# A hybrid attention and RG-LRU block: another order in the opening, with c spread by a transfer and the first shift summed on VectorE

## The chip, the cores and the metric

The kernel runs on one core of a Trainium2 chip. A core has TensorE (PE, matrix products), VectorE (DVE), ScalarE (ACT), GpSimd (POOL) and SyncE (SP, which here only issues transfers), and 16 DMA engines between its memory (SBUF) and HBM. The metric is the device time of one launch in microseconds.

## The reference, cut to what matters

```python
def rmsnorm(x, g):
    r = lax.rsqrt(jnp.mean(xf * xf, axis=-1, keepdims=True) + NORM_EPS)
    return (xf * r).astype(x.dtype) * g
...
    mod = c @ w_ada[l] + b_ada[l]                    # c: 1 x 1024
    shift, scale, gate = jnp.split(mod, 3, axis=-1)
    h = rmsnorm(x, norm_g[l]) * (1.0 + scale[:, None, :]) + shift[:, None, :]
    proj = h @ w_in[l]
    q, k, v, g_attn, xr, g_rnn, m_attn, m_rnn = jnp.split(proj, SPLIT_POINTS, axis=-1)
    ...  # rotary positions, windowed attention with sinks, convolution, RG-LRU
    merged = (jax.nn.sigmoid(m_attn) * (y_attn @ w_attn_proj[l])
              + jax.nn.sigmoid(m_rnn) * (y_rnn @ w_rnn_proj[l]))
    x = x + gate[:, None, :] * (merged @ w_out[l])
return rmsnorm(x, final_g)
```

x is 1024 rows (time) by 1024 features. The change concerns the way from x and c to h, and the first products that use h.

## The kernel before, in words

Products are made in three passes: each operand is split into a high part (a value rounded to the reduced matmul format) and a low part (the rest), and high by high, low weight by high, and high weight by low are added up. In names, `wh`/`wl` are the parts of a weight half, `hh`/`hl` those of h; `hha`/`hhb` are the two time halves of a chunk of `hh`. The products of the main projection that come after the opening use sums and differences of quarter blocks of h (`differences`, `make_operands`, the operands `nh` and `nl`) and run in line 690.

The opening works in this order. `manual_schedule` means that every engine executes its instructions exactly in program order; an instruction that waits holds up all behind it on its engine.

- Loads, on SyncE's queue in program order: the eight 128-row tiles of x (`xt`, 512 KB each), the packed small parameters `pk_t`, then halves of weights (`r`, 256 KB) and tiles of the shift and scale weights (`wada`, 512 KB, two for each of the eight 128-feature chunks of h) in the order of their use. `xt` and `wada` share 12 buffers. The two halves of the row c (`c_row_t`, 2 KB each) come on ScalarE's queue.
- TensorE is kept turning with products of zeros (`turn_array`, line 251), then spreads c over the 128 partitions by a product with a column of ones (line 259); VectorE copies that to `c_bc` (lines 420, 421).
- For each x tile i: `square(i)` sums the squares on ScalarE (line 360, with an accumulator read behind it), `mean(i)` divides and adds epsilon on VectorE (363), `root(i)` is on ScalarE (367), `scaled(i)` inverts on VectorE (371) and multiplies either the tile (373) or, for tiles 0, 2 and 4, an identity matrix (377). `flip(i)` transposes the tile's eight chunks on TensorE (lines 390 and 392) into one of two sets of four PSUM banks; two tiles share a set.
- `out_of(j, p, eng)` evicts bank p of tile pair j into `xT` (line 398 on ScalarE, 400 on VectorE). Pairs 0 and 2 are in one set of banks (`bk`), 1 and 3 in the other (the later accumulators `pmain`).
- The first chunk's shift is a sum over features by eight thin products (line 446, on weights laid out for that on the host), all other shifts and all scales are multiply-and-sum instructions on VectorE (`modulate`, line 270). Four more products of zeros follow (449, `KEEP_BUSY`).
- `scales_of(kc)` makes the two per-feature constants of chunk kc on ScalarE (275, 277). `hi_parts(kc)` makes from `xT` the high part in two halves (406; whole in 408 for chunks 4 to 7) and the full value (410) on ScalarE, with what is given as `between` in the middle. `lo_parts(kc)` makes the low part on VectorE (467, 470). `cast_s` and `rest_s` split the weight halves of the first four output blocks (101 on ScalarE or 219 on GpSimd, and 107 on VectorE).
- `first(kc, terms, cs)` multiplies chunk kc into the accumulators of the output blocks cs, in line 480: term "h" is high by high, "w" low weight by high, "l" high weight by low. The first products of all are those of chunk 0.

Behind the eight chunks, lines 1488 to 1523 interleave the last low parts, the differences and operands for the main products, the halves of the v weights (`half`), the rotary positions of the keys (`rope_a`, `rope_b`), which read and free the first accumulators, and two products for v (`v_product`, lines 1461 to 1463). GpSimd computes the angles of the rotary positions in small steps (`turn`).

Of the kernel before, what the change touches and what calls it, by code (L numbers as in the profile page):

```python
# [12 lines left out]
F32 = mybir.dt.float32  # L13
# [3 lines left out]
BF16 = mybir.dt.bfloat16  # L17
AF = mybir.ActivationFunctionType
ALU = mybir.AluOpType
# [26 lines left out]
SL = [slice(0, HALF), slice(HALF, S)]  # L46
XT = 12
DIAG = 0, 2, 4
KEEP_BUSY = 4


@with_exitstack
def tile_hybrid_block(ctx, tc, x, pk, rows, posr, posi, c_row, w_ss, w_gate, w_main, w_v,
# [32 lines left out]
    def pcol(base, i):  # L86
        return pk_t[:, base + i:base + i + 1]
# [97 lines left out]
    START = (0, 1, 34, 35)  # L185
    with ExitStack() as st:
        sp = st.enter_context(tc.tile_pool(name="start", bufs=1, side="right"))
        c_row_t = [wp.tile([P, HALF], F32, tag="ws", name="c_row_t", bufs=3)[0:1, :]
                   for _ in range(2)]
        for i in range(2):  # L190
            dma(c_row_t[i], c_row[:, SL[i]], A)
        posr_t = sp.tile([P, 65], I32, name="posr_t")
        dma(posr_t[:], posr, G)
        invf_t = posr_t[:, 64:65].bitcast(F32)
# [3 lines left out]
        for i in range(8):  # L198
            t = sp.tile([P, D], F32, tag="xt", name="xt", bufs=XT)
            dma(t[:], x[i * P:(i + 1) * P, :])  # L200
            xt.append(t)
        dma(pk_t[:], pk)

        def load_ss(kc):
# [18 lines left out]
        def rest_s(c, i):  # L223
            rest(sw[c][i], raw[c, i])
# [15 lines left out]
            load_ss(kc)  # L240
        rv = [load_half(w_v[i // 2][:, SL[i % 2]]) for i in range(4)]

        one_row = sp.tile([1, P], F32, name="one_row")
        warm = sp.tile([P, 1], F32, name="warm")
        V.memset(one_row[:], 1.0)
        zero = rbig[:, :HALF]
        V.memset(zero, 0.0)

        def turn_array(n):
            for i in range(n):  # L250
                T.matmul(bk[i % 2], zero[:, 0:P], zero, start=True, stop=True)  # L251

        V.memset(warm[:], 1.0)
        A.activation(warm[:], warm[:], AF.Sqrt)
        c_bc = sp.tile([P, D], F32, name="c_bc")
        psc = starts[0]
        turn_array(12)
        for hf in range(2):
            T.matmul(psc[hf], one_row[:], c_row_t[hf], start=True, stop=True)
        turn_array(2)  # L260

        mods = sp.tile([P, 16], F32, name="mods")
        gsc = sp.tile([P, 8], F32, name="gsc")
        shf = sp.tile([P, 8], F32, name="shf")
        bng = sp.tile([P, 8], F32, name="bng")

        def modulate(kc, which=(0, 1)):
            for a in which:
                jk = sp.tile([P, D], BF16, tag="junk2", name="jk")
                V.scalar_tensor_tensor(out=jk[:], in0=wada[kc, a][:], scalar=1.0, in1=c_bc[:],  # L270
                                       op0=ALU.mult, op1=ALU.mult,
                                       accum_out=mods[:, a * 8 + kc:a * 8 + kc + 1])

        def scales_of(kc):
            A.activation(shf[:, kc:kc + 1], mods[:, kc:kc + 1] if kc else bk[0][:, 0:1],
                         AF.Identity, bias=pcol(PK_BSH, kc))
            A.activation(gsc[:, kc:kc + 1], mods[:, 8 + kc:9 + kc], AF.Identity,
                         scale=pcol(PK_NG, kc), bias=bng[:, kc:kc + 1])

# [77 lines left out]
        junk_t = wp.tile([P, HALF], F32, tag="ws", name="junk", bufs=3)  # L357

        def square(i):
            A.activation(junk_t[:].bitcast(BF16), xt[i][:], AF.Square, accum_out=ss[:, i:i + 1])  # L360

        def mean(i):
            V.tensor_scalar(out=rr[:, i:i + 1], in0=ss[:, i:i + 1], scalar1=1.0 / D, scalar2=EPS,
                            op0=ALU.mult, op1=ALU.add)

        def root(i):
            A.activation(rr[:, i:i + 1], rr[:, i:i + 1], AF.Sqrt)

        def scaled(i):
            r1 = rr[:, i:i + 1]  # L370
# [49 lines left out]
        late = {1: [lambda: V.tensor_copy(c_bc[:, SL[0]], psc[0]),  # L420
                    lambda: V.tensor_copy(c_bc[:, SL[1]], psc[1])],
                3: [lambda: out_of(0, 0, V), lambda: out_of(0, 1, V)],
                4: [lambda: out_of(0, 2, V), lambda: out_of(0, 3, A)],
                5: [lambda: out_of(1, 0, V), lambda: out_of(1, 1, V)],
                6: [lambda: out_of(1, 2, A), lambda: out_of(1, 3, A),
                    lambda: V.scalar_tensor_tensor(
                    out=bng[:], in0=pk_t[:, PK_BSC:PK_BSC + 8], scalar=1.0,
                    in1=pk_t[:, PK_NG:PK_NG + 8], op0=ALU.add, op1=ALU.mult)]}
        for i in range(8):
            square(i)  # L430
            mean(i)
            if i:
                root(i - 1)
                scaled(i - 1)
                if i < 6:
                    turn(3)
                flip(i - 1)
            for f in late.get(i, ()):
                f()
        root(7)  # L440
        scaled(7)
        for p in range(4):
            out_of(2, p, A)
        flip(7)
        for k in range(KC):
            T.matmul(bk[0][:, 0:1], wada[0, 0][:, k * P:(k + 1) * P], pcol(PK_C, k),
                     start=(k == 0), stop=(k == KC - 1))
        for i in range(KEEP_BUSY):
            T.matmul(bk[1], zero[:, 0:P], zero, start=True, stop=True)
# [12 lines left out]
        csn = sp.tile([P, 3, 64], F32, name="csn")  # L462
# [28 lines left out]
        def more():  # L491
            out_of(3, 2, A)
            out_of(3, 3, A)
# [1005 lines left out]
    now(rope_a(lambda: starts[0][0], 0, to_k))  # L1499
    for c in range(2, 4):  # L1500
        for kc in (6, 7):
# [360 lines left out]
def arrange(inputs):  # L1862
    i = {k: np.asarray(v) for k, v in inputs.items()}
    w_in = i["w_in"][0]
    w_ada = i["w_ada"][0]
    b_ada = i["b_ada"][0]
    cw = i["conv_w"][0]
    a = {}
    a["x"] = np.ascontiguousarray(i["x"][0])
    a["pk"] = np.ascontiguousarray(np.concatenate(  # L1870
        [_pc(i["c"][0]), _pc(b_ada[:1024]), _pc(b_ada[1024:2048]), _pc(i["norm_g"][0])]
        + [_pc(cw[k]) for k in range(4)]
        + [_pc(i["conv_b"][0]), _pc(i["rg_ba"][0]), _pc(i["rg_bx"][0]), _pc(i["rg_lambda"][0])],
        axis=1))
# [9 lines left out]
    a["w_ss"][:128] = w_ada[:, :128].reshape(8, 128, 128).transpose(1, 0, 2).reshape(128, 1024)  # L1884
# [25 lines left out]
```

## Time and profile before

| | us |
|---|---|
| median of 3 runs | 927.20 |
| lowest and highest | 926.62, 927.23 |
| the profiled execution | 927.22 |
| its span, first to last instruction | 925.4 |
| TensorE busy in it | 916.5 |
| VectorE, ScalarE, GpSimd busy | 677.7, 544.2, 128.9 |
| first product of line 480 starts at | 23.44 |

The profile is of one execution. Its page gives the busy time of each engine and the costliest groups of instructions; questions to the trace give the instructions of a stretch in order of time (start, duration, engine, line, operation, output <- inputs, and in brackets the idle time before it with what ended it), who waited for whom, and sums over given stretches. A duration includes what an engine overlaps with its next instruction, so two neighbours can start closer together than the first one's duration.

### The profile page before, as it was taken

To read this page: it belongs to the slowest core of one execution; us is meant where nothing else is said; L and a number is where in the kernel's file an instruction comes from. 1 tells how busy PE (TensorE), PEld (TensorE's weight loads), DVE (VectorE), ACT (ScalarE), POOL (GpSimd) and SP (SyncE) were. 2 spreads that over 40 slices of the span, in tenths; PEclk is the share of its full clock that TensorE was granted. 3 is DMA by queue.
4 is the path that set the end of the run, shared out by engine and by line. 5 is a ranking of instruction groups with operands and counts; after the bars stand their busy time and mean duration, and the time that the engine had idled before them with its cause. 6 is when DMAs were issued, how large, how long until landed. Compare 5 with 4: busy or idle time off the path is not lost.

```text
span 925.4 us, 12505 instructions
## 1 busy us (share of the span) xinstructions
PE 916.5 (99%) x4318; PEld 757.0 (82%) x4319; DVE 677.7 (73%) x1000; ACT 544.2 (59%) x1056; POOL 128.9 (14%) x225
## 2 busy tenths in 40 slices
PE   9999999999999999999999999999999999999997
PEld 6789888888888888888888888888888788888886
DVE  6997685877659946876786787899999748656522
ACT  7956654645558664956585875888887522212311
POOL 6420332000000000000000001444353200000000
PEclk9999999999999999999999999999999999999999
DMA  9829377641334522363334367994754198545331
GB/s 359 320 84 284 117 233 236 201 148 63 100 111 142 193 87 91 117 202 92 114 125 148 103 223 267 339 371 167 236 180 154 62 375 308 181 151 197 98 131 69
DMA packets 79300, 166.04 MB, mean 179 GB/s; under 512 B 7891, under 2 KB 28387, under 8 KB 79237
## 3 DMA queue, kind: packets, MB, share of 16 engines
q1 hardware_dynamic: 75152, 152.38, 47.5%
q0 software_dynamic: 3936, 12.59, 4.4%
q8 instruction: 34, 0.56, 0.2%
q14 instruction: 30, 0.24, 0.1%
q10 hardware_dynamic: 148, 0.27, 0.1%
HBM read 114.00 MB, written 51.61 MB: 179 GB/s over the span
## 4 chain that ended last, share of the span: by engine, by line
PE 94%; DVE 4%; issue 1%; ACT 1%; POOL 0%; DVEq 0%; ACTq 0%
PE bk L690 47%; PE rp L168 13%; PE pmain L1764 5%; PE pgate L1003 5%; PE pmain L168 5%; PE rp L1764 4%; PE s_ps L1214 3%; PE bk L480 3%; PE pv L1287 2%; PE pmain L480 2%; PE pt L1253 1%; PE pmain L1461 1%; PE pmain L1462 1%; PE pmain L1463 1%; PE bk L251 1%
## 5 line engine op out<-in xcount | busy, mean ns | idle before, releaser
L690 PE MATMUL bk<-nh,wh 128*128 128x512 f32 x368 | 144.5, 393 | 0.0
L690 PE MATMUL bk<-nl,wh 128*128 128x512 f32 x368 | 144.1, 392 | 0.0
L690 PE MATMUL bk<-nh,wl 128*128 128x512 f32 x368 | 143.8, 391 | 0.0
L101 ACT CAST wh<-r 128x512 fp32r<-128x512 f32 x107 | 65.7, 618 | 38.3 <-DMA r<-w_ap 15.4
L107 DVE TENSOR_TENSOR wl<-r,wh 128x512 fp32r<-128x512 f32 x109 | 79.0, 732 | 6.3 <-ACT wh L101 6.3
L690 PEld LDWEIGHTS bk<-nl,wh 128*128 128x128 f32 x368 | 69.1, 188 | 15.5
L690 PEld LDWEIGHTS bk<-nh,wl 128*128 128x128 f32 x368 | 69.1, 188 | 15.1
L690 PEld LDWEIGHTS bk<-nh,wh 128*128 128x128 f32 x368 | 69.2, 188 | 14.6
L690 PE MATMUL bk<-hh,wh 128*128 128x512 f32 x184 | 72.2, 393 | 0.0
L690 PE MATMUL bk<-hl,wh 128*128 128x512 f32 x184 | 72.1, 392 | 0.0
L690 PE MATMUL bk<-hh,wl 128*128 128x512 f32 x184 | 71.9, 391 | 0.0
L107 DVE TENSOR_TENSOR wl<-ws,wh 128x512 fp32r<-128x512 f32 x76 | 51.5, 684 | 4.8 <-ACT wh L101 4.8
L1239 ACT ACTIVATE p<-p,small 128x129 f32<-128x129 f32 x128 | 50.1, 401 | 0.0
L101 ACT CAST wh<-ws 128x512 fp32r<-128x512 f32 x76 | 45.7, 615 | 3.1 <-DVE ws L712 1.5
L690 PEld LDWEIGHTS bk<-hl,wh 128*128 128x128 f32 x184 | 34.6, 188 | 7.8
L690 PEld LDWEIGHTS bk<-hh,wl 128*128 128x128 f32 x184 | 34.6, 188 | 7.5
L690 PEld LDWEIGHTS bk<-hh,wh 128*128 128x128 f32 x184 | 34.6, 188 | 7.3
L1214 PE MATMUL s_ps<-ks,qs 128*128 128x256 f32 (+1 forms) x256 | 37.6, 289 | 0.1
L868 POOL MEMSET xr<- 128x3 f32 x8 | 0.8, 101 | 259.7 <-PE pgate L1003 233.0
L803 ACT ACTIVATE c<-bk 128x512 f32<-128x512 f32 x29 | 17.3, 597 | 32.6 <-PE bk L690 32.6
L690 PE MATMUL bk<-hha,wl 128*128 128x512 f32 x92 | 36.1, 393 | 0.2 <-DVE wl L107 0.2
L690 PE MATMUL bk<-hha,wh 128*128 128x512 f32 x92 | 36.1, 393 | 0.0
(365 smaller groups left out, 2283.3 us busy)
## 6 DMA issues: line engine op xcount, KB each, us to landing
r<-w_main SPq DMA_DIRECT2D x100, 256.0 KB, 4.2
wada<-w_ss SPq DMA_DIRECT2D x16, 512.0 KB, 9.1
qs<-q_d SPq DMA_DIRECT2D x16, 512.0 KB, 5.5
ks<-k_d SPq DMA_DIRECT2D x12, 384.0 KB, 3.5
xt<-x SPq DMA_DIRECT2D x8, 512.0 KB, 6.9
sma_d<-c SPq DMA_DIRECT2D x16, 256.0 KB, 3.3
q_d<-rhi SPq DMA_DIRECT2D x16, 256.0 KB, 4.0
q_d<-rlo SPq DMA_DIRECT2D x16, 256.0 KB, 4.2
```

The lines of the kernel that those rows point to most:

```text
L101: A.copy(dst[0][:], src)
L107: V.tensor_tensor(out=dst[1][:], in0=src, in1=f32(dst[0][:]), op=ALU.subtract)
L168: mm = T.matmul(ps[hf], ww, xx[kc][hf], start=(kc == 0 and ww is w_h and xx is xh), stop=(kc == KC - 1 and xx is xl))
L251: T.matmul(bk[i % 2], zero[:, 0:P], zero, start=True, stop=True)
L480: T.matmul(starts[c][hf], ww[:, c0:c0 + P], xh[kc][hf], start=(kc == 0 and t_ == "h"), stop=(kc == KC - 1 and t_ == "l"))
L690: W["pe"] = T.matmul(ps, ww[:, c], b[kc][xx_], start=(first and kc == 0 and i == 0), stop=(kc == 3 and i == 2), skip_group_check=not first)
L803: A.activation(t["t"], s(), AF.Tanh, scale=0.5)
L1003: W["pe"] = T.matmul(ps[:, SL[hf]], ww[:, c0:c0 + P], xx_[:, SL[hf]], start=(ic == 0 and i == 0), stop=(ic == 1 and i == 2))
L1214: W["pe"] = T.matmul(o, qs[:, j, qc], ks[:, kb:n % 2 + 2, b, :], start=(b == 0), stop=(b == 1))
L1239: A.activation(px[:, j, :], px[:, j, :], AF.Exp, bias=sm[:, 0, j:j + 1], accum_out=sm[:, 1, j:j + 1])
L1287: W["pe"] = T.matmul(pv[:], b, m[:].rearrange("p j q -> p (j q)"), start=(i == 0), stop=(i == len(prods) - 1))
L1764: T.matmul(ps[:, sl], lhs[k][th][:, ts_], w[:, sl], start=(k == 0 and w is h_ and lhs is mh), stop=(k == KC - 1 and lhs is ml))
```

## The change

`c` comes as one transfer that spreads its row over the partitions (512 KB into SBUF, on SyncE's queue behind x); the thin transfers, the products with ones and the two copies go. `mean` goes; `root` takes 1/D as its scale and a tile of epsilon as its bias. Tile 3 is squared on VectorE. Chunk 0's shift is summed by `modulate` like the others, with the weights in their usual layout, and the eight thin products go. `KEEP_BUSY` is 11 instead of 4. The loop over x tiles is written out: each root stands right behind its square, and evictions stand elsewhere; all four of pair 3 come ahead of the first `hi_parts`, and the casts of blocks 0 and 1 both stand inside it. The first products go through chunks 0 and 1 in another order. Later, `make_operands(0)` stands behind `lo_parts(7)`, and `differences(1)` behind the last half of v's weights. In the written-out part several statements share a line here.

```diff
-KEEP_BUSY = 4
+KEEP_BUSY = 11
+ON_V = 3,
...
-        for i in range(2):
-            dma(c_row_t[i], c_row[:, SL[i]], A)
...
+        c_bc = sp.tile([P, D], F32, name="c_bc")
+        dma(c_bc[:], c_row.to_broadcast([P, D]))
         dma(pk_t[:], pk)
...
-        V.memset(warm[:], 1.0)
-        A.activation(warm[:], warm[:], AF.Sqrt)
-        turn_array(12)
-        for hf in range(2):
-            T.matmul(psc[hf], one_row[:], c_row_t[hf], start=True, stop=True)
-        turn_array(2)
+        V.memset(warm[:], EPS)
+        A.activation(mods[:, 0:1], warm[:], AF.Sqrt)
+        turn_array(16)
...
         def square(i):
+            if i in ON_V:
+                jk = sp.tile([P, D], BF16, tag="junk2", name="jk")
+                V.scalar_tensor_tensor(out=jk[:], in0=xt[i][:], scalar=1.0, in1=xt[i][:],
+                                       op0=ALU.mult, op1=ALU.mult, accum_out=ss[:, i:i + 1])
+                return
             A.activation(junk_t[:].bitcast(BF16), xt[i][:], AF.Square, accum_out=ss[:, i:i + 1])
-        def mean(i):
-            V.tensor_scalar(out=rr[:, i:i + 1], in0=ss[:, i:i + 1], scalar1=1.0 / D, scalar2=EPS,
-                            op0=ALU.mult, op1=ALU.add)
         def root(i):
-            A.activation(rr[:, i:i + 1], rr[:, i:i + 1], AF.Sqrt)
+            A.activation(rr[:, i:i + 1], ss[:, i:i + 1], AF.Sqrt, scale=1.0 / D, bias=warm[:])
...
-        for i in range(8):
-            square(i)
-            mean(i)
-            if i:
-                root(i - 1)
-                scaled(i - 1)
-                ...
-                flip(i - 1)
-            for f in late.get(i, ()):
-                f()
+        square(0); root(0); scaled(0); flip(0)
+        square(1); root(1); scaled(1); turn(3); flip(1)
+        square(2); root(2); scaled(2); turn(3); flip(2)
+        square(3); square(4); root(3); root(4)
+        out_of(0, 0, V); scaled(3); out_of(0, 1, V); turn(3); flip(3)
+        out_of(0, 2, V); out_of(0, 3, A); scaled(4); turn(3); flip(4)
+        square(5); root(5); scaled(5); out_of(1, 0, V); out_of(1, 1, V); turn(3); flip(5)
+        square(6); root(6); out_of(1, 2, A); out_of(1, 3, A); scaled(6); flip(6)
+        square(7)
         root(7)
         scaled(7)
+        V.scalar_tensor_tensor(out=bng[:], ...)
         for p in range(4):
             out_of(2, p, A)
         flip(7)
-        for k in range(KC):
-            T.matmul(bk[0][:, 0:1], wada[0, 0][:, k * P:(k + 1) * P], pcol(PK_C, k),
-                     start=(k == 0), stop=(k == KC - 1))
-        for i in range(KEEP_BUSY):
-            T.matmul(bk[1], zero[:, 0:P], zero, start=True, stop=True)
+        turn_array(KEEP_BUSY)
         for c in (2, 3):
             cast_s(c, 0, G)
-        cast_s(0, 0)
         turn()
-        modulate(0, (1,))
-        for p in range(2):
+        modulate(0)
+        for p in range(4):
             out_of(3, p, A)
         scales_of(0)
-        hi_parts(0, lambda: cast_s(1, 0))
-        for c in (2, 3, 0):
+        hi_parts(0, lambda: [cast_s(c, 0) for c in (0, 1)])
+        for c in (2, 3):
             rest_s(c, 0)
         modulate(1)
...
-        for t_ in "hw":
-            first(0, t_, (2, 3, 0))
         scales_of(1)
-        hi_parts(1, more)                     # more: out_of(3, 2, A), out_of(3, 3, A)
-        rest_s(1, 0)
-        for t_ in "hw":
-            first(1, t_, (2, 3, 0))
-        for t_ in "hw":
-            for kc in range(2):
-                first(kc, t_, (1,))
+        hi_parts(1)
+        for c in (0, 1):
+            rest_s(c, 0)
+        first(0, "h", (2, 3, 0, 1))
+        first(0, "w", (2, 3))
+        first(1, "h", (2, 3, 0, 1))
+        first(0, "w", (0, 1))
+        first(1, "w", (2, 3, 0, 1))
         lo_parts(0)
...
     differences(0)
-    make_operands(0)
     chunks(5)
     lo_parts(7)
+    make_operands(0)
...
-    wv = [half(rv[0])]
-    differences(1)
-    wv.append(half(rv[1]))
+    wv = [half(rv[0]), half(rv[1])]
...
     wv.append(half(rv[3]))
+    differences(1)
     v_product(0)
```

More of the change, by code (lines that the diff above doesn't have):

```diff
@@ L187, in tile_hybrid_block @@
         sp = st.enter_context(tc.tile_pool(name="start", bufs=1, side="right"))
-        c_row_t = [wp.tile([P, HALF], F32, tag="ws", name="c_row_t", bufs=3)[0:1, :]
-                   for _ in range(2)]
-        for i in range(2):
-            dma(c_row_t[i], c_row[:, SL[i]], A)
         posr_t = sp.tile([P, 65], I32, name="posr_t")
@@ L241, in tile_hybrid_block @@
         rv = [load_half(w_v[i // 2][:, SL[i % 2]]) for i in range(4)]
-        one_row = sp.tile([1, P], F32, name="one_row")
         warm = sp.tile([P, 1], F32, name="warm")
-        V.memset(one_row[:], 1.0)
         zero = rbig[:, :HALF]
@@ L251, in turn_array @@
                 T.matmul(bk[i % 2], zero[:, 0:P], zero, start=True, stop=True)
-        V.memset(warm[:], 1.0)
-        A.activation(warm[:], warm[:], AF.Sqrt)
-        c_bc = sp.tile([P, D], F32, name="c_bc")
-        psc = starts[0]
-        turn_array(12)
-        for hf in range(2):
-            T.matmul(psc[hf], one_row[:], c_row_t[hf], start=True, stop=True)
-        turn_array(2)
         mods = sp.tile([P, 16], F32, name="mods")
+        V.memset(warm[:], EPS)
+        A.activation(mods[:, 0:1], warm[:], AF.Sqrt)
+        turn_array(16)
         gsc = sp.tile([P, 8], F32, name="gsc")
@@ L265, in tile_hybrid_block, with modulate @@
         bng = sp.tile([P, 8], F32, name="bng")
-        def modulate(kc, which=(0, 1)):
-            for a in which:
+        def modulate(kc):
+            for a in (0, 1):
                 jk = sp.tile([P, D], BF16, tag="junk2", name="jk")
@@ L274, in scales_of @@
         def scales_of(kc):
-            A.activation(shf[:, kc:kc + 1], mods[:, kc:kc + 1] if kc else bk[0][:, 0:1],
-                         AF.Identity, bias=pcol(PK_BSH, kc))
+            A.activation(shf[:, kc:kc + 1], mods[:, kc:kc + 1], AF.Identity, bias=pcol(PK_BSH, kc))
             A.activation(gsc[:, kc:kc + 1], mods[:, 8 + kc:9 + kc], AF.Identity,
@@ L419, in tile_hybrid_block @@
         turn(3)
[L420 to L428, printed above, removed]
-        for i in range(8):
-            square(i)
-            mean(i)
-            if i:
-                root(i - 1)
-                scaled(i - 1)
-                if i < 6:
-                    turn(3)
-                flip(i - 1)
-            for f in late.get(i, ()):
-                f()
+        square(0)
+        root(0)
+        scaled(0)
+        flip(0)
+        square(1)
+        root(1)
+        scaled(1)
+        turn(3)
+        flip(1)
+        square(2)
+        root(2)
+        scaled(2)
+        turn(3)
+        flip(2)
+        square(3)
+        square(4)
+        root(3)
+        root(4)
+        out_of(0, 0, V)
+        scaled(3)
+        out_of(0, 1, V)
+        turn(3)
+        flip(3)
+        out_of(0, 2, V)
+        out_of(0, 3, A)
+        scaled(4)
+        turn(3)
+        flip(4)
+        square(5)
+        root(5)
+        scaled(5)
+        out_of(1, 0, V)
+        out_of(1, 1, V)
+        turn(3)
+        flip(5)
+        square(6)
+        root(6)
+        out_of(1, 2, A)
+        out_of(1, 3, A)
+        scaled(6)
+        flip(6)
+        square(7)
         root(7)
         scaled(7)
+        V.scalar_tensor_tensor(out=bng[:], in0=pk_t[:, PK_BSC:PK_BSC + 8], scalar=1.0,
+                               in1=pk_t[:, PK_NG:PK_NG + 8], op0=ALU.add, op1=ALU.mult)
         for p in range(4):
@@ L485, in chunks @@
                 first(kc, terms, (c,))
-        for t_ in "hw":
-            first(0, t_, (2, 3, 0))
         scales_of(1)
-        def more():
-            out_of(3, 2, A)
-            out_of(3, 3, A)
-        hi_parts(1, more)
-        rest_s(1, 0)
-        for t_ in "hw":
-            first(1, t_, (2, 3, 0))
-        for t_ in "hw":
-            for kc in range(2):
-                first(kc, t_, (1,))
+        hi_parts(1)
[6 more added lines that the diff above has]
+        first(1, "w", (2, 3, 0, 1))
         lo_parts(0)
@@ L1883, in arrange @@
     a["w_ss"] = np.ascontiguousarray(w_ada[:, :2048].T)
-    a["w_ss"][:128] = w_ada[:, :128].reshape(8, 128, 128).transpose(1, 0, 2).reshape(128, 1024)
     a["w_gate"] = np.ascontiguousarray(w_ada[:, 2048:])
```

## The prediction

> **What bounds the kernel now.** I read the page first, then who TensorE waited for, then TensorE's own instructions around its first real products, and from there back along ScalarE, VectorE and the transfers. The page:
>
> ```profile
> span 925.4 us, 12505 instructions
> PE 916.5 (99%) x4318; PEld 757.0 (82%) x4319; DVE 677.7 (73%) x1000; ACT 544.2 (59%) x1056; POOL 128.9 (14%) x225
> ```
>
> TensorE is busy for 916.5 of 925.4 us. Its waits, longest first:
>
> ```profile
> PE bk L251 <- DVE warm L253: 1.4, 1, 1.4
> PE bk L480 <- ACT hha L406: 0.7, 1, 0.7
> ...
> PE bk L690 <- DVE wl L107: 0.2, 1, 0.2
> ```
>
> So after the first product of normalized h (line 480), TensorE practically never stops again. The change touches none of the products that follow, so it can move the end only by moving the time at which this unbroken stream gets under way. TensorE there:
>
> ```profile
> 18.23 1.97 PE L390 MATMUL pmain<-ident,xt 128*128 128x128 f32 x16
> 20.03 1.84 PE L446 MATMUL bk<-pk_t,wada 128*128 128x1 f32 x16
> 21.73 1.02 PE L449 MATMUL bk<-rbig 128*128 128x512 bf16 x3
> 23.44 0.77 PE L480 MATMUL bk<-hha,wh 128*128 128x512 f32 x1 [0.68 <-ACT hha L406]
> 24.64 0.63 PE L480 MATMUL bk<-hha,wh 128*128 128x512 f32 x1
> 25.07 0.63 PE L480 MATMUL bk<-hhb,wh 128*128 128x512 f32 x1
> 27.88 0.40 PE L480 MATMUL bk<-hha,wh 128*128 128x512 f32 x1
> 28.11 0.40 PE L480 MATMUL bk<-hhb,wh 128*128 128x512 f32 x1
> ```
>
> The first product starts at 23.44. Products then start 0.43 us apart (24.64, 25.07), later 0.23 (27.88, 28.11). The stretches show why:
>
> ```profile
> 16.30:19.70 3.40, 3.21 (x27) 1.00 1.04 401
> 19.70:23.20 3.50, 3.00 (x24) 1.00 1.02 404
> 23.20:26.60 3.40, 3.16 (x7) 0.50 1.04 402
> 26.60:30.00 3.40, 3.40 (x16) 0.99 1.02 403
> ```
>
> Columns: length, TensorE busy with its count, granted clock, DMA share, GB/s. The clock was half in 23.2 to 26.6 and full around it; the transfers run at some 400 GB/s throughout, so 512 KB take 1.3 us.
>
> The mark by which I compare is the 14th product, at 28.11: it is the first that takes the second half of chunk 1 of h. From there the before stream runs at 0.23 without a gap.
>
> **The change, part by part.** ScalarE sets when h appears:
>
> ```profile
> 7.86 1.06 ACT L360 ACTIVATE junk<-xt 128x1024 bf16<-128x1024 f32 x1 [1.01 <-DMA xt<-x]
> 10.43 1.06 ACT L360 ACTIVATE junk<-xt 128x1024 bf16<-128x1024 f32 x1
> 11.40 0.19 ACT L360 ACTIVATION_READ_ACCUMULATOR junk<-xt 128x1 f32 x1
> 11.91 0.59 ACT L398 COPY xT<-bk 128x512 f32<-128x512 f32 x1 [0.23 <-PE bk L390]
> 16.98 0.53 ACT L367 ACTIVATE rr<-rr 128x1 f32<-128x1 f32 x2
> 17.82 2.06 ACT L398 COPY xT<-bk 128x512 f32<-128x512 f32 x4 [0.30 <-PE bk L390]
> 21.91 0.26 ACT L275 ACTIVATE shf<-bk,pk_t 128x1 f32<-128x1 f32 x1 [0.55 <-PE bk L446]
> 22.07 0.38 ACT L277 ACTIVATE gsc<-mods,bng,pk_t 128x1 f32<-128x1 f32 x1
> 22.48 0.81 ACT L406 ACTIVATE hha<-xT,shf,gsc 128x512 fp32r<-128x512 f32 x1
> 23.90 0.60 ACT L101 CAST wh<-r 128x512 fp32r<-128x512 f32 x1
> 24.41 1.24 ACT L410 ACTIVATE xT<-xT,shf,gsc 128x1024 f32<-128x1024 f32 x1
> 26.87 0.81 ACT L406 ACTIVATE hhb<-xT,shf,gsc 128x512 fp32r<-128x512 f32 x1
> ```
>
> *One square less on ScalarE.* It saves 1.06 + 0.19 us, but ahead of tile 4, whose square starts at 10.43 when its rows arrive: tiles land 1.3 us apart, tile 2 at 7.8 (it was waited for 1.01 us), so tile 4 at 10.4. The time saved becomes waiting for tile 4. Gain: 0.
>
> *Mean folded into the root.* Each root now follows its own square on ScalarE and must wait for the accumulator read (0.19) to end instead of starting 0.1 into it, and it has a tensor for its bias, as line 275 has (0.26 against 0.19). I charge 0.2 us a tile. From 10.43 to the end of the last root, ScalarE still does four squares, five roots and three evictions. Before, that took 10.43 to 17.51 (16.98 + 0.53). After: a square takes 0.97 to its accumulator read (10.43 to 11.40), the read 0.19, the root behind it 0.22 up to the next issue, so 1.38 a tile for tiles 5 and 6; tile 4 with roots 3 and 4 takes 1.45, tile 7 up to the end of its root 1.47; the evictions take 0.50, and 1.03 for two. Sum 7.21, end 17.64. In it the stall of 0.23 at 11.91 and its like are already gone, since the evictions now ask for banks long written. Delta +0.13. VectorE saves eight tiny means and gets the square (1.3, placed by line 270 below), which ends near 11.1, ahead of the root that needs it (11.5).
>
> *From the last root to the first h.* The root at 17.64 lets VectorE invert and scale tile 7 (line 373 below; to 18.62), the eight flips of tile 7 follow (1.1, the half that the first eviction needs at 19.4), while ScalarE evicts group 2, 17.55 to 19.63. Then come all four evictions of group 3 at 0.52, to 21.70; before only two stood here, with a cast (0.51) that now comes later. The two scale instructions take 0.60 to the first h: 22.30, against 22.48. The 16 thin matmuls of line 446 go, and with them the 0.55 that ScalarE waited for them; the extra eviction takes 0.52 of it back. Delta −0.31, and with the +0.13 the first h is 0.18 us earlier.
>
> *First shift on VectorE.* What follows there:
>
> ```profile
> 18.28 0.75 DVE L373 TENSOR_SCALAR xt<-xt,rr 128x1024 f32<-128x1024 f32 x1
> 18.95 1.26 DVE L270 SCALAR_TENSOR_TENSOR jk<-wada,c_bc 128x1024 bf16<-128x1024 f32 x1
> 38.02 0.68 DVE L467 TENSOR_TENSOR hlb<-xT,hhb 128x512 fp32r<-128x512 f32 x1
> 42.65 0.40 PE L480 MATMUL pmain<-hla,wh 128*128 128x512 f32 x1
> 57.81 1.22 DVE L470 TENSOR_TENSOR hl<-xT,hh 128x1024 fp32r<-128x1024 f32 x1
> 75.96 0.69 DVE L629 TENSOR_TENSOR rlo<-pmain,rhi 128x512 fp32r<-128x512 f32 x1 [1.26 <-DMA k_d<-rlo]
> L1461 PE MATMUL pmain<-wh,hhb x16: 281/283/283, 80.6 to 88.8; 128*128 128x256 f32 x16
> ```
>
> Tile 7 is scaled by 18.6, the small sum for the scales takes 0.2, two sums of 1.26 end at 21.3; ScalarE asks at 21.9. Cover 0.6 us; beyond it each microsecond counts fully. Everything behind on VectorE is up to 1.2 us later relative to h, but it is needed late: the low part of chunk 3 ended at 38.70 and is first read at 42.65. Cost 0.
>
> *Two casts behind the first h instead of one.* The gap from first h to the halves of chunk 1 grows by one cast, 0.51: the last half ended 5.20 after the start of the first (27.68 against 22.48); it will end 5.70 after, at 28.00. The stream finds chunk 1 not ready: at full clock twelve products at 0.23 from 23.26 on are through by about 26.2, so a new wait of about one microsecond appears, on ScalarE. The 14th product comes at 28.00 + 0.14 = 28.14. Even twelve products at half clock (5.1 us from 23.26) are only 0.3 later, so clearing the slow stretch gains almost nothing: what it cost before is the time that chunk 1 now takes.
>
> *Eleven idle matmuls instead of four* fill 2.4 us after tile 7's flips, 19.8 to 22.2, in front of 23.26: free at full clock. At half clock (0.43) they end near 24.5.
>
> *c by DMA.* Four matmuls, two copies and two tiny transfers vanish from stretches that bounded nothing; 512 KB more enter the load queue behind x, ahead of all weights.
>
> ```profile
> wo<-w_out SPq DMA_DIRECT2D x1, 512.0 KB, 3.4
> fg_bc<-rows SPq DMA_DIRECT2D x1, 512.0 KB, 5.2
> 832.60:834.60 2.00, 2.00 (x11) 1.62 (x10) 1.89 (x2) 0.57 (x1) 0.00 (x0) 1.00 0.69 221
> ```
>
> (Columns: count, size, us from issue to landing; then a stretch as above.) The kernel has one such spread row elsewhere, fg_bc: 5.2 us to landing against 3.4 for a plain load of that size, and only 221 GB/s while it ran. So it costs 1.3 us (a plain 512 KB) to 3.1 (1.3 + 1.8). At 221 in place of 402 GB/s the 2 us lost 0.9, which gives 2.2; I take that. Chunk 0's second load landed before its sum at 18.95, and by bytes at 18.3; its sum would end at 18.3 + 2.2 + 1.26 = 21.8, just inside ScalarE's 21.9. Cost 0, without reserve: from 2.3 us on, each microsecond counts. The weight casts on GpSimd move 2.2 later too; their reader, VectorE, comes to them only behind the two sums.
>
> *Differences of h.* The low part of chunk 7 ended at 59.03 and now comes 2.3 earlier. The differences of chunk 1 (four subtractions of some 0.7, as line 467 takes) move behind the halves of v and ahead of the last reads of the key accumulators, which ended at 76.65; that becomes some 77.8. The second v product needs them at 80.6. Cost 0.
>
> **Sum.** +0.13 − 0.31 + 0.21 (the 0.51 of the cast, less the 0.3 by which before had chunk 1 ready too early) = +0.03 us. The profiled execution took 927.22 us (span 925.4), the runs' median is 927.2, so no correction: 927.2.
>
> [...]
>
> **Rivals.** *Slow stretch later.* If the half clock falls behind the 14th product, 3.4 us there hold 8 products instead of 15, 7 × 0.23 = 1.6 us: 928.8. For it: a wait of one microsecond now stands at 26 to 27. Against: eleven fillers, where 19.7 to 23.2 had three recorded and 16 thin ones. [...]
>
> *Slower: the spread row delays the weights.* With 3.1 us for c, chunk 0's sum ends at 22.7, the first h starts 0.46 later (scale constant and hand-over), chunk 1 is whole 5.70 after that, and the 14th product comes at 29.0, 0.9 late: 928.1. The mechanism decides from 2.3 us, and exceeds what can be measured from 4.1. For it: fg_bc's 5.2; against: that row was partly queued behind another load.
>
> *Faster: x arrives earlier.* Tile 2 kept ScalarE waiting for 1.01 us, although 512 KB take only 1.3. If the two removed transfers of c on ScalarE's queue caused it, all later x tiles come 1.0 earlier and the chain with them: 926.2. Against: those were 2 KB each.
>
> *The opening does what it seems to,* and chunk 1 is not late because VectorE and ScalarE overlap better than I placed them: up to 0.5 faster, 926.7; inside the forecast's own ±0.5.
>
> **How the numbers follow.** Forecast 0.62, slow stretch 0.12, slow c 0.13 (0.03 of it above 4.1 us), earlier x 0.13. A change under 0.2% (1.85 us), about what a measurement of this kernel can tell from no change, holds nearly all: 0.88. Slower by more needs c above 4.1 or a slow stretch and a slow c together, 0.07; faster by more needs x earlier and the roots cheaper than charged, 0.05. Range: 926.0 (x earlier, roots at 0) to 928.9 (slow stretch).
>
> **What would show it.** Right: tile 4's square still at 10.4; last root near 17.6; first h near 22.3; a wait of about 1 us of TensorE on ScalarE's second chunk; 14th product near 28.1; no new wait after it. Wrong: VectorE's first two sums waiting for a load; a half clock after 28; TensorE waiting on a low part or the key accumulators between 30 and 81.

## The result, and the profile after

| | before | after |
|---|---|---|
| median of 14 runs, us | 927.30 | 929.03 |
| lowest and highest | 925.93, 928.16 | 928.05, 930.98 |
| the profiled execution, its span | 927.22, 925.4 | 929.57, 927.8 |
| TensorE busy in it | 916.5 | 914.6 |
| 14th product of the opening starts at | 28.11 | 28.47 |

The changed kernel takes 1.002 times as long, with a 95% interval of 1.0011 to 1.0028: 1.7 us slower. The forecast of 927.2 was wrong, and the median lies just above the range's upper end of 928.9.

The head of the changed kernel's page, and behind it the list of TensorE's waits, longest first (who waits, for whom, us in total, times, the longest). In this list and in those below, rows in between are left out:

```profile
span 927.8 us, 12468 instructions
PE 914.6 (99%) x4307; PEld 754.3 (81%) x4308; DVE 678.5 (73%) x993; ACT 544.3 (59%) x1054; POOL 130.5 (14%) x225
```

```profile
PE bk L491 <- ACT hha L398: 2.4, 2, 1.8
...
PE bk L696 <- ACT bk L748: 0.8, 1, 0.8
...
PE bk L696 <- DVE wl L108: 0.4, 1, 0.4
...
PE bk L696 <- DVE wl L110: 0.2, 1, 0.2
```

Lines 491 and 696 are the 480 and 690 of before. The prediction expected the waits of line 491 and no new ones behind them. What it did not expect are those of line 696, the main products, long after the opening: TensorE waits for ScalarE's copy of a bank (748) and for VectorE's low parts (108, 110). Before, line 690 had one wait, of 0.2 us, for a low part; the other two are new.

**The opening went nearly as written.** ScalarE, VectorE and TensorE in order of time, after the change:

```profile
10.30 1.06 ACT L356 ACTIVATE junk<-xt 128x1024 bf16<-128x1024 f32 x1 [1.11 <-DMA xt<-x]
17.08 0.29 ACT L359 ACTIVATE rr<-ss,warm 128x1 f32<-128x1 f32 x1
19.10 1.22 DVE L262 SCALAR_TENSOR_TENSOR jk<-wada,c_bc 128x1024 bf16<-128x1024 f32 x1 [0.25 <-DMA wada<-w_ss]
21.02 1.22 DVE L262 SCALAR_TENSOR_TENSOR jk<-wada,c_bc 128x1024 bf16<-128x1024 f32 x1 [0.69 <-DMA wada<-w_ss]
22.29 0.39 ACT L268 ACTIVATE gsc<-mods,bng,pk_t 128x1 f32<-128x1 f32 x1 [0.72 <-DVE jk L262]
22.71 0.81 ACT L398 ACTIVATE hha<-xT,shf,gsc 128x512 fp32r<-128x512 f32 x1
23.67 0.47 PE L491 MATMUL bk<-hha,wh 128*128 128x512 f32 x1 [1.78 <-ACT hha L398]
27.76 0.49 PE L491 MATMUL bk<-hha,wh 128*128 128x512 f32 x1 [0.65 <-ACT hha L398]
28.47 0.50 PE L491 MATMUL bk<-hhb,wh 128*128 128x512 f32 x1 [0.21 <-ACT hhb L398]
```

The last root ends at 17.37 (forecast 17.64), but the two sums of VectorE each wait for a load, which was one of the prediction's own signs of being wrong; the second ends at 22.24, and ScalarE waits 0.72 us for it. The first h starts at 22.71 instead of 22.30 and the 14th product comes 0.36 us late.

**The late part lost the rest.** VectorE before, where the four subtractions of `differences(1)` stand between the low parts of the first two halves of v's weights, and further on the key part before the last:

```profile
59.55 0.68 DVE L555 TENSOR_TENSOR xT<-xT 128x512 f32<-128x512 f32 x1
...
61.72 0.69 DVE L558 TENSOR_TENSOR xT<-xT 128x512 f32<-128x512 f32 x1
62.33 0.68 DVE L107 TENSOR_TENSOR wl<-r,wh 128x512 fp32r<-128x512 f32 x1
...
74.02 0.68 DVE L629 TENSOR_TENSOR rlo<-pmain,rhi 128x512 fp32r<-128x512 f32 x1
```

And after:

```profile
60.43 0.68 DVE L108 TENSOR_TENSOR wl<-r,wh 128x512 fp32r<-128x512 f32 x1
62.31 0.69 DVE L108 TENSOR_TENSOR wl<-r,wh 128x512 fp32r<-128x512 f32 x1 [1.20 <-ACT wh L102]
63.56 0.69 DVE L616 TENSOR_TENSOR c<-pmain,ctab 128x512 f32<-128x512 f32 x1 [0.56 <-ACT c L615]
71.92 0.68 DVE L561 TENSOR_TENSOR xT<-xT 128x512 f32<-128x512 f32 x1
...
77.04 0.68 DVE L635 TENSOR_TENSOR rlo<-pmain,rhi 128x512 fp32r<-128x512 f32 x1
78.38 0.69 DVE L635 TENSOR_TENSOR rlo<-pmain,rhi 128x512 fp32r<-128x512 f32 x1 [0.66 <-ACT rhi L631]
```

Before, the low part of the second half ran at 62.33 with no wait shown: the subtractions ahead of it filled the time in which ScalarE had not yet cast that half (the cast ran from 61.22 to 61.84). After, the same low part runs at 62.31, no earlier, with 1.20 us of waiting ahead of it. The subtractions start at 71.92 and delay what follows: the last two key parts run at 77.04 and 78.38, where before they ran at 74.02 and 75.96.

What hangs on that, in two lists, before first (SyncE's queue issues a transfer at the time given; the rest as above):

```profile
80.04 2.15 SPq L60 DMA_DIRECT2D r<-w_main  x3
86.19 0.69 DVE L712 TENSOR_TENSOR ws<-r 128x512 f32<-128x512 f32 x1 [1.38 <-DMA r<-w_main]
92.18 0.59 ACT L1468 COPY vv<-pmain 128x512 f32<-128x512 f32 x1 [3.63 <-PE pmain L1463]
94.93 0.59 ACT L1468 COPY vv<-pmain 128x512 f32<-128x512 f32 x1 [2.16 <-DMA v_d<-vv]
```

After:

```profile
82.40 2.13 SPq L61 DMA_DIRECT2D r<-w_main  x3
88.57 0.69 DVE L718 TENSOR_TENSOR ws<-r 128x512 f32<-128x512 f32 x1 [0.74 <-DMA r<-w_main]
92.50 0.69 DVE L718 TENSOR_TENSOR ws<-ws,r 128x512 f32<-128x512 f32 x1 [0.37 <-DMA v_d<-vv]
93.11 0.68 DVE L110 SCALAR_TENSOR_TENSOR wl<-ws,wh 128x512 fp32r<-128x512 f32 x1
93.88 0.59 ACT L1474 COPY vv<-pmain 128x512 f32<-128x512 f32 x1 [3.58 <-DVE wl L110]
97.11 0.59 ACT L1474 COPY vv<-pmain 128x512 f32<-128x512 f32 x1 [2.65 <-DMA v_d<-vv]
98.13 0.59 ACT L748 COPY bk<-bk 128x512 f32<-128x512 f32 x1
98.77 0.50 PE L696 MATMUL bk<-nh,wh 128*128 128x512 f32 x1 [0.84 <-ACT bk L748]
```

The key stores wait on SyncE's in-order queue for the key parts: the store of the part before the last is issued at 77.75, as soon as that part has ended, and before at 74.73. The loads of the first main weights (`w_main`) stand behind the key stores: 82.40 instead of 80.04. The first store of v stands behind those loads, at 86.83 instead of 84.74. VectorE's first sum of these weights comes 2.38 us later. Its second sum, at 92.50, also has to wait for that store of v to land, since the sums and the copies of v share three buffers, and its low part ends at 93.79. ScalarE's copy of v needs such a buffer too and now waits for VectorE instead of TensorE, its next copy waits for the store of the one before, and behind that on ScalarE stands the bank copy (748) that TensorE needs: one product starts at 97.53, the next at 98.77, of which the profile puts 0.84 us down to the wait. Smaller waits follow at 110.53 (0.18) and 130.43 (0.38, where before had 0.15 at 128.49).

As a second mark I take the first product of line 690 or 696 behind the wait near 128 (or, where there is none, the product in its place): 128.49 before, 130.43 after. Of the 1.94 us, 0.36 come from the opening and 1.58 from the stretch between the marks. The spans of the two executions differ by 2.4 us; the rest comes behind the second mark, where the trace names no wait for it.

### The profile page after: what moved, and what is told of

Its sections match the earlier page's. It is cut to its first block, busy times and chain, and to the rows that moved or that the text cites. A ratio compares the mean times of both kernels' runs of the same rounds, so it can differ in the third digit from the quotient of the medians.

```text
span 927.8 us, 12468 instructions
## 1 busy us (share of the span) xinstructions
PE 914.6 (99%) x4307; PEld 754.3 (81%) x4308; DVE 678.5 (73%) x993; ACT 544.3 (59%) x1054; POOL 130.5 (14%) x225
## 4 chain that ended last, share of the span: by engine, by line
PE 87%; DMA 5%; DVE 4%; ACT 2%; issue 1%; SPq 0%; POOL 0%; DVEq 0%; ACTq 0%; POOLq 0%
PE bk L696 46%; PE rp L169 13%; PE pmain L1769 5%; PE pgate L1009 5%; PE pmain L169 5%; PE rp L1769 4%; PE s_ps L1220 3%; PE pv L1293 2%; PE pmain L491 2%; PE bk L491 2%; PE pt L1259 1%; DMA v_d<-vv 1%; DMA wada<-w_ss 1%; DMA xt<-x 1%; DMA k_d<-rlo 1%
## 5 line engine op out<-in xcount | busy, mean ns | idle before, releaser
L1786 ACT ACTIVATE o<-xo 128x1024 f32<-128x1024 f32 (+2 forms) x10 | 8.9, 889 | 46.7 <-DVE xo L1785 44.2
```

## The experiments

Each kernel was timed beside the kernel before on the same chip, and the ratio is to that (its median was 927.65 beside e1 to e4, 927.76 beside e5 to e9, 927.41 beside f1 and f2). "Stretch" is from the 14th product to the second mark in the one profiled execution. Two executions of the same program, e6 and f2, differ in it by 0.78 us, so only differences above that are read from one execution alone.

| kernel | median us | ratio to before, 95% | 14th product | second mark | stretch |
|---|---|---|---|---|---|
| before | 927.30 | | 28.11 | 128.49 | 100.38 |
| after | 929.03 | 1.0020 (1.0011 to 1.0028) | 28.47 | 130.43 | 101.96 |
| e1_diff_back | 927.58 | 1.0002 (0.9992 to 1.0012) | 28.62 | 129.34 | 100.72 |
| e2_only_diff | 929.03 | 1.0017 (1.0007 to 1.0027) | 27.57 | 129.29 | 101.72 |
| e3_loads_first | 928.10 | 1.0010 (1.0001 to 1.0019) | 28.44 | 129.66 | 101.22 |
| e4_shift_load_first | 928.89 | 1.0020 (1.0010 to 1.0029) | 27.89 | 129.99 | 102.10 |
| e5_back_and_shift_first | 928.27 | 1.0006 (0.9998 to 1.0015) | 27.96 | 129.35 | 101.39 |
| e6_also_main_loads_first | 926.37 | 0.9994 (0.9985 to 1.0003) | 27.87 | 128.18 | 100.31 |
| e8_all_diff_back | 927.30 | 0.9998 (0.9988 to 1.0008) | 28.43 | 129.29 | 100.86 |
| e9_key_stores_early | 930.11 | 1.0038 (1.0024 to 1.0051) | 27.95 | 131.78 | 103.83 |
| f1_before_main_loads_first | 926.37 | 0.9991 (0.9983 to 1.0000) | 29.05 | 128.82 | 99.77 |
| f2_best_again | 926.63 | 0.9991 (0.9982 to 1.0000) | 27.97 | 129.06 | 101.09 |

The theory: the moved `differences(1)` costs the time, because it filled a wait of VectorE and now delays the key parts and what is queued behind them. The rival: the opening costs it, by c's transfer and the later first h.

**e1_diff_back: the changed kernel with `differences(1)` back in its old place.**

```diff
-    wv = [half(rv[0]), half(rv[1])]
+    wv = [half(rv[0])]
+    differences(1)
+    wv.append(half(rv[1]))
...
     wv.append(half(rv[3]))
-    differences(1)
     v_product(0)
```

> The changed kernel with one edit: the differences of chunk 1 stand again between the first and second half of v's weights. Marks: start of the first product after the wait near 128.5 us (before 128.49, after 130.43) and of the 14th product (28.11 and 28.47). Theory A (the moved differences hold up the last key stores, behind them the next weight loads and the second v store, and through ScalarE's queue a product): the wait of 1.2 us near 98 goes, the late mark falls to about 128.9 (128.49 + the 0.36 of the opening), time about 927.6. Theory B (c's spread row delays all loads, and the waits near 98 to 130 follow from that): the late mark stays near 130.4, time 929. Theory C (the two executions differ by the pitch of the products alone): time as before the edit, 929.

The time is back at that of before: 1.0002. TensorE's only wait of line 696 in the list of waits, and from the timeline the issue of the weight loads:

```profile
PE bk L696 <- DVE wl L108: 0.3, 1, 0.3
```

```profile
81.16 2.19 SPq L61 DMA_DIRECT2D r<-w_main  x3
```

The wait for the bank copy is gone from the list, and the loads are issued 1.24 us earlier than in the changed kernel. In its timeline the key part before the last runs at 75.25, 1.79 us earlier than in the changed kernel; the last one runs at 77.76, only 0.62 earlier, because it now waits 1.83 us for an earlier key store. The opening kept its changes here, and its 14th product is even a little later. That speaks for the theory and leaves the rival nothing that can be measured.

**e2_only_diff: the kernel before with this one move and nothing else.** The edit is that of e1 the other way round, on the kernel before.

> The kernel before with one edit: the differences of chunk 1 moved behind the last half of v's weights, nothing else. Theory A: opening as before (14th product 28.1), a wait of about 1 us near 97 to 98, late mark about 130.0, time 1.5 above before, 928.8. Theory B and C: late mark 128.5, time as before, 927.3.

1.0017, its interval above 1: the move alone makes the old kernel slower, by 1.4 us in the medians (929.03 against 927.65 beside it). From its timeline, the issue of the weight loads and the product behind the first late wait:

```profile
81.77 2.15 SPq L60 DMA_DIRECT2D r<-w_main  x3
...
97.91 0.50 PE L690 MATMUL bk<-nh,wh 128*128 128x512 f32 x1 [0.44 <-ACT bk L742]
```

The same wait for the bank copy (742 here) appears that was not there before, and the loads are issued at 81.77 instead of 80.04, though the opening of this execution was 0.5 us earlier. With e1 this settles which part of the change costs the time.

**e3_loads_first: the changed kernel with the loads of the first main weights (`begin`) issued ahead of the key stores.** It takes away one link of the chain, the queue.

```diff
-    for hf in range(2):
-        now(rope_b(lambda: starts[1][hf], hf, to_k))
     begin(-6)
     begin(-5)
+    for hf in range(2):
+        now(rope_b(lambda: starts[1][hf], hf, to_k))
```

> The changed kernel with one edit: the three loads for the first main products are issued ahead of the last key stores on SyncE's queue. Theory A with the queue as the link: loads land at about 76 to 79 instead of 87 to 88.5, v's stores land earlier, the wait near 98 goes, late mark about 129, time about 927.7, although the differences still stand late. If the link is VectorE's and ScalarE's own time, not the queue: late mark 130 to 130.4, time 929. Theory B: no change either, 929.

The issue of the loads in its timeline, and the only wait of line 696 in its list of waits:

```profile
73.30 2.55 SPq L61 DMA_DIRECT2D r<-w_main  x3
```

```profile
PE bk L696 <- DVE wl L108: 0.3, 1, 0.3
```

The loads go out at 73.30 instead of 82.40, the wait near 98 is gone, and the median is 0.9 us below that of the changed kernel, though the two intervals (1.0001 to 1.0019, 1.0011 to 1.0028) overlap. So the queue is a link of the chain; the size of that link is not settled. What is left (1.0010) shows in the trace as TensorE waiting 0.35 us for VectorE's low part ahead of 129.66.

**e4_shift_load_first: the changed kernel with chunk 0's two `wada` tiles loaded ahead of the first weight halves,** so that the late spread row no longer keeps VectorE waiting.

```diff
+        load_ss(0)
         for c in (2, 3):
             load_s(c, 0)
-        load_ss(0)
```

> The changed kernel with one edit: the two loads for the first shift and scale stand ahead of the first weight halves instead of behind them. If c's spread row is what made the first h late (its sums waited 0.9 us for loads): these loads land 1.3 us earlier, the sums wait for nothing, the first h starts at 22.2 to 22.3 (22.71), the 14th product at about 28.1 (28.47), late mark about 130.0 under theory A; time 0.4 lower, below what the timing can tell. If ScalarE's own work bounds the first h: no change at 22.7 and 28.5.

Its timeline, and the wait for the bank copy in its list of waits:

```profile
21.29 0.81 ACT L398 ACTIVATE hha<-xT,shf,gsc 128x512 fp32r<-128x512 f32 x1
27.18 0.49 PE L491 MATMUL bk<-hha,wh 128*128 128x512 f32 x1 [1.49 <-ACT hha L398]
```

```profile
PE bk L696 <- ACT bk L748: 0.6, 1, 0.6
```

The first h starts at 21.29, 1.42 us earlier, but the 14th product only 0.58 earlier: the wait for chunk 1 grows to 1.49 us, since the loads of its own shift and scale (VectorE waits 0.89 us for one at 23.34) now end last. The total does not move (1.0020), and the wait for the bank copy is still there. A faster opening did not repair the late part.

**e5_back_and_shift_first: e1 and e4 together.**

> The changed kernel with two edits: the differences of chunk 1 back between the first two halves of v's weights, and the two loads for the first shift and scale ahead of the first weight halves. If the late differences (1.4 us) and the loads behind c's spread row (0.4 to 0.5) are the whole loss and add up: first h at 22.2, 14th product near 28.0, wait near 98 at most 0.3, product after the wait near 128.5 at about 128.9, time about 927.2, that is 0.4 below the edit of the differences alone. If the two overlap (the opening's gain is eaten by the waits near 98 to 129): product at 129.3, 927.6.

1.0006, an interval on both sides of 1. The 14th product is about as early as in e4, but a new wait of 0.19 us stands ahead of 69.55, where a v product waits for VectorE's rotation (616), and one of 0.23 ahead of 109.85 for a low part. Inconclusive as to a gain.

**e6_also_main_loads_first: e5 with the loads of e3, and f2_best_again, the same kernel once more.**

> As the kernel with both of these edits, and the three loads for the first main products ahead of the last key stores. If the queue of SyncE is what is left of the waits near 98 and 110: these go, product at 128.5 to 128.7, time about 926.9. If what is left is the chain of v's stores and loads behind the second v product, which starts with TensorE's own end: waits near 110 and 129 stay at 0.2 to 0.5, 927.2.

> The best kernel so far once more, beside the kernel before on one chip: the changed opening with the first shift's loads ahead, the differences of chunk 1 back, the main loads ahead of the last key stores. If its gain is real: 14th product near 27.9, no wait near 98 or 110, product after the wait near 128.2, time 0.4 to 1.4 below before. If it was chance: within 0.3 of before.

926.37 and 926.63, ratios of 0.9994 (0.9985 to 1.0003) and 0.9991 (0.9982 to 1.0000). Both intervals reach 1.0000, so a gain of 0.1% is not shown by either alone. In e6 the loads go out at 73.71, and the trace shows no wait of TensorE from 30 to 135. In f2 one of 0.34 is back ahead of 129.06.

**e8_all_diff_back: e1 with `make_operands(0)` back in its old place too.**

> The changed kernel with both edits of the later order undone: the differences of chunk 1 back, and the operands of chunk 0 again ahead of the low part of chunk 7. What is left against the kernel before is the opening alone. If the place of the operands of chunk 0 costs something too: waits near 98 and 110, 0.2 each with only the differences put back, go, product after the wait near 128.5 at 128.9, time 0.3 to 0.5 under that kernel's 927.6. If it is neutral, as the prediction had it: waits and times as with the differences alone.

0.9998, e1's within the interval: the place of `make_operands(0)` is neutral. This kernel differs from before in the opening alone, so the opening neither gains nor costs what can be measured.

**e9_key_stores_early: e4 with `differences(1)` and `make_operands(1)` moved further, behind the key stores and the loads.**

```diff
     wv.append(half(rv[3]))
-    differences(1)
     v_product(0)
-    make_operands(1)
     for hf in range(2):
         now(rope_b(lambda: starts[1][hf], hf, to_k))
     begin(-6)
     begin(-5)
+    differences(1)
+    make_operands(1)
```

> The changed kernel with the differences and operands of chunk 1 put behind the last key stores instead of ahead of them, and the loads for the first shift and scale first. If it is the lateness of the key stores on SyncE's queue that costs, not the place of the differences as such: the last key part ends at about 73 to 75 (78.38), the loads for the main products are issued by 76 to 78 (82.40), no wait near 98, product after the wait near 128.5 at 128.5 to 128.9, time about 927.0. If VectorE's and ScalarE's sum of work up to 98 costs: waits as in the changed kernel, 0.6 to 1.0 near 98, 928.5.

This kernel is the slowest of all, 1.0038. Its last two key parts are earlier than in the changed kernel (71.49 and 76.67, against 77.04 and 78.38), but the last one has a wait of its own, as the timeline shows. The list of TensorE's waits shows what else changed:

```profile
76.67 0.69 DVE L635 TENSOR_TENSOR rlo<-pmain,rhi 128x512 fp32r<-128x512 f32 x1 [4.50 <-DMA k_d<-rlo]
```

```profile
PE bk L696 <- DVE wl L110: 2.0, 1, 2.0
```

VectorE stands 4.50 us until an earlier key store has freed its buffer, with the subtractions now queued behind it instead of ahead of it, where they would have filled the wait. The low part for which TensorE then waits runs at 93.50, where the changed kernel has it at 91.45. The weight loads were issued at 80.13, as early as in the kernel before (80.04), so early loads alone do not help: VectorE's own order is a second link, beside SyncE's queue.

**f1_before_main_loads_first: the kernel before with e3's order of loads and stores and nothing else.**

> The kernel before with one edit: the three loads for the first main products ahead of the last key stores. If the load order alone brings what the best kernel so far gained (926.4 with the changed opening): loads land near 78 to 80 instead of 85 to 86, the wait near 128.5 (0.3) shrinks, time 926.5 to 927.2. If the changed opening has a part in it: no wait to remove near 98, so product after the wait at 128.5 as before, time 927.5.

926.37, 0.9991 (0.9983 to 1.0000), with the loads at 74.28 instead of 80.04 in the timeline:

```profile
74.28 1.71 SPq L60 DMA_DIRECT2D r<-w_main  x3
```

This is one edit, and it is as fast as e6 and f2 with the whole changed opening: about 0.1%, at the edge of what these runs can tell. So the changed opening adds nothing that shows to the order of loads.

## Why the prediction was wrong, point by point

- *One square less on ScalarE:* right. Tile 4's square starts at 10.30 (forecast 10.4); the time saved became a wait of 1.11 us for tile 4.
- *Mean folded into the root:* right; the last root ends 0.27 earlier than worked out, 0.13 of it because tile 4 started that much earlier than in the kernel before. A root runs behind its accumulator read, at 17.08 after a read that ends at 17.05, so 0.2 a tile was a little too much.
- *First shift on VectorE* and *c by DMA:* the mechanism was right, the term was mis-sized. The forecast had the sum end at 21.8 "without reserve"; it ended at 22.24, and the first h came at 22.71 instead of 22.30. The stretch while c was spread, before and then after (length, the engines' busy times with counts, clock, DMA share, GB/s):

```profile
13.20:14.20 1.00, 0.81 (x8) 0.62 (x7) 1.00 (x2) 1.00 (x4) 0.93 (x2) 1.00 1.06 401
14.20:15.20 1.00, 1.00 (x9) 0.80 (x8) 0.96 (x5) 0.84 (x4) 0.31 (x2) 1.00 1.07 418
15.20:16.20 1.00, 1.00 (x11) 1.00 (x10) 0.97 (x4) 1.00 (x3) 0.96 (x2) 1.00 1.04 414
```

```profile
13.20:14.20 1.00, 0.57 (x6) 0.34 (x4) 0.96 (x5) 0.97 (x4) 0.76 (x4) 1.00 1.01 307
14.20:15.20 1.00, 0.93 (x8) 0.93 (x9) 0.96 (x4) 0.97 (x4) 0.96 (x1) 1.00 0.83 224
15.20:16.20 1.00, 1.00 (x12) 1.00 (x11) 1.00 (x3) 1.00 (x3) 0.70 (x2) 1.00 0.97 356
```

  At 307, 224 and 356 GB/s, where 401, 418 and 414 were moved before, some 0.35 MB are lost, 0.8 us at 411 GB/s. With the 1.3 us for the bytes themselves that is 2.1 us, and 2.2 was taken. Chunk 0's two loads agree for the first: it landed at 19.0, 2.0 later than before (17.0). The second landed at 20.93, 2.6 later than before (18.3, as the step had it). So the price of the transfer was about right, and what the sum lacked is that the second load fell another 0.6 us behind the first; these rows do not show why, and no run tried it alone. The step also overlooked that the kernel has a second spread row, `bg`, which took 5.7 us to landing where fg_bc took 5.2 (both in the trace of before).
- *Two casts behind the first h:* right. The last product of chunk 0 starts at 26.72 and the first of chunk 1 at 27.76; the profile puts 0.65 us of that down to the new wait, where about 1 was forecast.
- *Eleven idle matmuls:* the clock was full through this opening (1.00 from 6 to 34 us). Whether they cause that is not shown: e1 has the same eleven and fell to half clock (0.50). The prediction priced twelve products at half clock at 0.3 us; e1's 14th product, with a half clock from 24.5 to 27.9, is 0.15 behind that of the changed kernel at full clock.
- *Differences of h:* **this is the step that failed.** It ends with "that becomes some 77.8. The second v product needs them at 80.6. Cost 0." The measured cost is 1.4 us where the move is made alone (e2), and nearly the whole loss is gone where it is taken back (e1). The step shows no working for 77.8. It took the low part of chunk 7 to come 2.3 us earlier, and it came 0.8 earlier (it ends at 58.24, before at 59.03). The last key part ended at 79.07, a delay of 2.4 us and not 1.2, and the part before it, for which the store queue waits, came 3.0 us later. The four subtractions (2.9 us) no longer fill a wait that the step had not looked for (1.20 and 0.56 us of idle VectorE in their old place): against e1, which has the same opening, taking them out there brought the last low part of v's weights forward by only 0.8 us (71.32 instead of 72.11). And the step followed the delay only to one reader, the v product. It did not ask what is queued behind the key parts: their stores on SyncE, the weight loads behind those, ScalarE's copies behind the store of v. The prediction's own list of signs named a wait for "the key accumulators between 30 and 81"; the waits stand at 98, 110 and 130, out of the stretch in which it looked.
- *The rivals.* "Slow stretch later" gave 928.8, near the measured time, but that is chance, for the reason is another: in the profiled execution the changed kernel's granted clock is 1.00 in every stretch of 3.4 us from 20 to 924 us. "The spread row delays the weights" is there with 0.36 us of the 0.9 that it was priced at. "x arrives earlier" did not happen: tile 2's square starts at 7.71 instead of 7.86 and tile 4's at 10.30 instead of 10.43, and the wait for tile 2 became one for tile 4. None of them named the moved subtractions.

## What to carry to other kernels

Before you move a step off a place, ask what wait of its engine it fills there: here a step of 2.9 us cost only 0.8 us in its old place, since it filled waits there, and moved it made the key part for which the stores wait 1.8 us later (the changed kernel against e1). Follow a delay through the queues behind it (stores that wait, loads behind these stores, copies behind a wait on the next engine), not only to the nearest reader of the data. A load with free buffers belongs ahead of stores that still wait for their data; in this kernel that order is worth about 0.1%, at the edge of what these runs can tell, and the changed opening nothing that these runs could measure.

## What the runs showed of the hardware that was not expected

**With one and the same opening the half-clock stretch comes or not.** Stretches of length, TensorE busy with its count, granted clock, DMA share, GB/s: first the changed kernel; then e1, with the same opening; then e2, with the opening of before, which ran at half clock there in the execution that the prediction shows; then f1, with the opening of before again:

```profile
23.20:26.60 3.40, 2.79 (x11) 1.00 1.03 402
```

```profile
24.50:27.90 3.40, 3.40 (x9) 0.50 1.04 401
```

```profile
23.20:26.60 3.40, 3.17 (x12) 1.00 1.04 402
```

```profile
24.20:27.60 3.40, 3.28 (x7) 0.50 1.04 408
```

In the executions of before, f1 and e1 the granted clock has such a stretch in the opening (0.50 for 3.4 us from 23.2, 24.2 and 24.5). In those of the changed kernel, e2, e3, e4, e6 and e8 it is 1.00 from 19.7 to 30.0, though before, e2 and f1 share one opening and the changed kernel, e1, e3 and e8 another. So in these executions the stretch comes or not, and changes its place. What sets its place is not shown. It costs little here: from the first product to the 14th it took 4.67 us in before and 4.73 in f1 with a half clock, and 4.29 in e2 without one. The mark itself moves more than that, from 27.57 in e2 to 29.05 in f1, but 1.04 us of this was there at the first product already (23.28 and 24.32) and on ScalarE at the first h (22.32 and 23.36), ahead of the half clock. So this mark cannot be read finer than some 1.5 us from one execution alone, and the 0.36 us by which the changed opening was late lies inside the scatter of the opening of before.

**A half clock far behind the opening.** In one execution, e9, a half-clock stretch (0.50 from 95.3 to 98.7) stands behind a pause of TensorE: one product starts at 91.83, the next at 94.23, with 2.01 us put down to the wait. Before and the changed kernel have none between 30 and 920 us (1.00 in every stretch of 3.4 us). Whether the pause is its cause is not shown: behind the waits of 1.78 us ahead of 23.67 in the changed kernel and of 1.49 us ahead of 27.18 in e4 the clock stays at 1.00 up to 30.0.
